# A two-layer transformer step: splits moved from GpSimd to VectorE, norm scales moved into the choice of experts, and gathered expert rows put into one buffer pool with the streamed table

## The chip, the cores and the metric

The kernel runs on one core of one Trainium2 chip. The metric is the device time of one execution in microseconds. The engines are named as in the profile: PE (TensorE matmul), PEld (its weight load), DVE (VectorE), ACT (ScalarE), POOL (GpSimd), SP (SyncE, which issues most DMAs).

## The reference, cut to what matters

Two layers work on 256 latent rows and 256 context rows of width 1024. Layer 0 mixes by attention and retention, layer 1 by a delta rule. After each mixer comes a layer norm and then `peer`: a lookup of 16 experts out of 16384 for each row and each of 8 heads, and after it another layer norm. `peer` is where most of the time goes:

```python
def block(xb):                                    # 128 rows
    q = (xb @ w_q).reshape(128, 8, 2, 128)
    s1, s2 = q[:, :, 0] . k1, q[:, :, 1] . k2     # 128 keys each
    v1, i1 = top_k(s1, 16); v2, i2 = top_k(s2, 16)
    cand = v1[..., :, None] + v2[..., None, :]
    sc, j = top_k(cand, 16)
    e_idx = ...                                    # 16 experts of i1 * 128 + i2
    gate = softmax(sc)
    act = gelu(einsum('phkd,pd->phk', u_tab[e_idx], xb))
    return einsum('phk,phkd->pd', gate * act, v_tab[e_idx])

xl = layer_norm(ALPHA * xl + g1 * yl, ln1_g[l], ln1_b[l])
fl = peer(modulate(xl, sh2, sc2), ...)
xl = layer_norm(ALPHA * xl + g2 * fl, ln2_g[l], ln2_b[l])
```

All of it is float32. The kernel gets that precision from float32r matmuls by splitting each operand x into a high part h = round(x) and a low part l = x - h, and adding three products (hh, hl, lh).

## The kernel before, in words

**Splits.** `split` writes the high part on ACT (tile names end in h: `arwh`, `ush`, `vsh`, `gsh`) and the low part by a subtraction with two SBUF operands on DVE or POOL (`arwl`, `usl`, `vsl`, `gsl`).

**First mixer** (0 to 190 us). 16 weight tiles `arw` and 4 tiles `rvw` are loaded, split and multiplied with the modulated input. Their low parts are computed on POOL (`eng=nc.gpsimd`). Beside them DVE computes `ada_unit`: the modulation vectors, one dot product of a 128x1024 tile with the condition for each of two streams (`adaj`, 48 of them here). `weave` interleaves the generators; the last part, `ret_v`, runs by itself after them. `w_out` is split on DVE and POOL in turn, and the modulated inputs (`hp0l`) alternate between the two too.

**Choice of experts** (`route`, 377 to about 700 us in layer 0; 2160 to 2370 us in layer 1). The query weights `wq` and the first chunks of table u are split on POOL here. DVE does the top-16 searches. The result is a dense weight table `wd` that goes through memory, and for row block 3 of layer 0 a list of expert numbers.

**Dense part of layer 0** (`Dense.run`, 716 to 1708 us). The tables u and v are streamed as 128 chunks of 128 experts. In the program's order each chunk c has: the load `ur` (512 KB) and its split, the product `act` with the activations, a `gelu`, the multiplication with the weights `w4`, its split `gsl`; the load `vr` (512 KB), its split `vsl`, and the product `f`. The first 36 chunks had their `act` done during the choice, so from 716 to 885 us there is only f. These are three of the four row blocks.

**Row block 3 of layer 0** goes another way: `Rows.steps` takes the 128 chosen experts of every row one at a time. For each of 128 steps POOL issues an indirect DMA of 512 KB from u (`rowu`, one expert row for each of 128 rows), DVE makes its dot product with the activations (`rowu`, then a read of the accumulator, `rowa`); 8 steps later (LAG) POOL gathers the same expert's row of v (`rowv`) and DVE adds it with its weight to the sum (`rowy`). A step is: multiply rowu s, issue gather of rowu s+RING[0], issue gather of rowv s-LAG+RING[1], add rowv s-LAG. The u rows have a ring of 4 buffers and the v rows one of 3 (RING = 4, 3), each its own; the `vr` chunks have 2 of the same size.

**The order.** The dictionary `fill` says at which chunk a step of the rows, an ada unit of layer 1 or something else is put; `at(share)` turns a share of the cost of all chunks into a chunk number. The scheduler that builds the program sets each engine's order and gives buffers to tiles as they are released in that order. `affine`, put at share 0.4, multiplies and adds the scale and shift of the first norm to x on POOL (lines 425 and 426 of the kernel before); layer 1 has another one at chunk 2.

Of the kernel before, what the change touches and what calls it, by code (L numbers as in the profile page):

```python
# [10 lines left out]
F32 = mybir.dt.float32  # L11
# [4 lines left out]
AF = mybir.ActivationFunctionType  # L16
# [5 lines left out]
P = 128  # L22
D = 1024
KD = D // P
# [22 lines left out]
AHEAD = 1  # L47
RING = 4, 3
LAG = 8
# [193 lines left out]
class Model:  # L243
# [186 lines left out]
    def modulate(self, pool, ps, l, m, x, s, hs, i0, ln):  # L430
        nc = self.nc
        sl = slice(i0 * P, (i0 + 2) * P)
        g, b = (self.c["ln_c"][:, ln[0], ln[1] - 1, z, :] for z in range(2))
        sc = pool.tile([P, KD], F32, tag="msc", name=f"msc{l}{m}{s}", bufs=2)
        sh = pool.tile([P, KD], F32, tag="msh", name=f"msh{l}{m}{s}", bufs=2)
        nc.vector.tensor_mul(sc, self.mod[l, m + 1][:, :, s], g)
        nc.vector.tensor_mul(sh, self.mod[l, m + 1][:, :, s], b)
        nc.vector.tensor_add(sh, sh, self.mod[l, m][:, :, s])
        for k in range(KD):
            self.n += 1  # L440
            o = ps.tile([P, 512], F32, tag="ps", name=f"xt{self.n}")
            for i in range(2):
                nc.tensor.transpose(o[:, i * P:(i + 1) * P], x[2 * s + i][:, k * P:(k + 1) * P], self.c["ident"])
            t = pool.tile([P, T], F32, tag="hf", name=f"hf{self.n}", bufs=3)
            nc.vector.tensor_scalar(t, o[:, :T], sc[:, k:k + 1], sh[:, k:k + 1], ALU.mult, ALU.add)
            nc.scalar.copy(hs[0][:, k, sl], t)
            (nc.gpsimd if k % 2 else nc.vector).tensor_sub(hs[1][:, k, sl], t, hs[0][:, k, sl].bitcast(F32))

# [19 lines left out]
    def mixer0(self, open_x, open_h):  # L468
# [25 lines left out]
        def weights(src, shape, nm):  # L494
            w = pw.tile(shape, F32, tag="w", name=nm, bufs=2)
            nc.sync.dma_start(w, src)
            return self.split(pw, w, shape, "arw", eng=nc.gpsimd)

# [120 lines left out]
        with ExitStack() as e2:  # L619
            pa = self.pool(e2, "m0ada2", 1, side="right")  # L620
            self.silu_rows(pa)

            def units():
                for m in (2, 3, 4):
                    for k in range(KD):
                        self.ada_unit(pa, 0, m, k, (0, 1))
                        yield

            weave(low(), pipe([key()] + [ret_proj(j) for j in range(4, 16)], 2), units())
            weave(ret_v())  # L630
        ep.close()
# [142 lines left out]
        with ExitStack() as e2:  # L774
            p = self.pool(e2, "m0o", 1, side="right")
            w = []
            for k in range(KD):
                r = p.tile([P, D], F32, tag="woutr", name=f"woutr{k}", bufs=3)
                nc.sync.dma_start(r, a["ar_out"][:, k, :])
                w.append(self.split(p, r, [P, D], f"wout{k}", eng=nc.gpsimd if k % 3 == 2 else nc.vector))  # L780
                next(rest, None)
# [30 lines left out]

    def route(self, l, hs, parts, ps, first, dense, e2, rows=None):
        nc, a, c = self.nc, self.a, self.c
# [15 lines left out]
        kT = p.tile([P, 16, P], F32, tag="A", name=f"kT{l}")  # L830
        nc.sync.dma_start(kT, a["p_k"][l])

        def top16(pool, vals, v, i, n, nm):
# [11 lines left out]
        def step(n):  # L845
            for _ in range(n):
                next(beside, None)
# [41 lines left out]
        def choose(part):  # L889
            n = 0  # L890
            pr = pipe([project(part, j) for j in range(16)], 2)
            for _ in range(2 * AHEAD):
                next(pr)
                yield
            tp = chain.from_iterable(top(part, j) for j in range(16))
            while True:
                ends = [next(g, pr) is pr for g in (pr, tp)]
                if all(ends):
                    return
                if ends[0]:  # L900
                    n += 1
                    step(1 + n % 2)
                yield

# [109 lines left out]
        for part in range(len(parts)):  # L1014
            weave(choose(part))
        eq_.close()
        dense.by = None
# [15 lines left out]
    class Rows:  # L1033
# [22 lines left out]

        def steps(self, pool):
            m, nc = self.m, self.m.nc
# [3 lines left out]
            def gather(z, s):  # L1062
                if 0 <= s < P:
                    t = rows[z, s] = pool.tile([P, D], F32, tag="row" + "uv"[z], name=f"row{'uv'[z]}{s}", bufs=RING[z])
                    nc.gpsimd.indirect_dma_start(t, None, tabs[z], bass.IndirectOffsetOnAxis(ap=self.e[:, s:s + 1], axis=0))  # L1065
# [20 lines left out]
    class Dense:  # L1086
# [61 lines left out]
        def run(self, wd, pool, psa, psv, fill, sums=None, ready=None):  # L1148
# [6 lines left out]
            def fetch(c):  # L1155
                late = c >= NE - 2
                vr = (self.p if late else pool).tile([P, D], F32, tag="ur" if late else "vr", name=f"vr{l}{c}", bufs=2)
                nc.sync.dma_start(vr, m.a["p_v"][l, c])
                if KEEP <= c < done:
                    self.gelu(c, None)  # L1160
                return vr
# [502 lines left out]
def build(nc, tc, a, out, dbg=None, upto="all"):  # L1664
    es = ExitStack()
    with es:
# [38 lines left out]
        dense = m.Dense(m, 0, h, 3, *pools0, EARLY[0])  # L1705
        wd = m.route(0, h, ((0, 1, 2, 3),), ps, first, dense, e2, rows)
        ep.close()
        psa = m.pool(e2, "psa0", 2, PSUM)
        psm = Tags(psa, ps=(psa, "act", 2))
        pools = (m.pool(e2, "densew0", 1), psa, m.pool(e2, "psv0", 1, PSUM))  # L1710
        steps = rows.steps(m.pool(ed, "rowring", 1, side="right"))
        ea = ExitStack()
# [3 lines left out]
        fill = {}  # L1716
        cost = np.cumsum([18 if c < EARLY[0] else 36 for c in range(NE - 6)])

# [6 lines left out]
        for i, u in enumerate(units):  # L1725
            n = 3 * KD
            share = ahead_share * (0.1 + 0.9 * i / n) if i < n else ahead_share + (0.97 - ahead_share) * (i - n) / (len(units) - n)
            fill.setdefault(at(share), []).append(lambda u=u: m.ada_unit(pa, *u))
        kept = {}

        def affine():
            rows = m.norm_rows(pa, 0, 1, "adat")
            for t in x[:4]:
                m.affine(nc.gpsimd, t, rows)

# [3 lines left out]

        fill.setdefault(at(0.4), []).append(affine)  # L1740
        fill[0] = [lambda: m.silu_rows(pa)]
        fill[124] = [prepare]
        for i in range(P + LAG):
# [5 lines left out]

        pm = Tags(m.pool(ed, "mod1", 1, side="right"), lnz=(pools[0], "w4", 2), hf=(pools[0], "vr", 2))  # L1750
        m.norm_modulate(pm, psm, (0, 2), (1, 0), x, (0, 1), ys, kept, h)
# [13 lines left out]
        with ed:  # L1765
            ep, ps = phase("r1ps")
            dense = m.Dense(m, 1, h, 2, *pools1, EARLY[1])
            wd = m.route(1, h, ((0, 1),), ps, first, dense, e2)
            ep.close()
# [6 lines left out]

            def affine():
                rows = m.norm_rows(pn, 1, 1)
                for t in x[2:4]:
                    m.affine(nc.gpsimd, t, rows)  # L1780

            last = dense.run(wd, *pools, {2: [affine]})
            for tb in range(2):
# [20 lines left out]
```

## Time and profile before

| | us |
|---|---|
| median of 3 runs | 3058.61 (3046.81 to 3059.09) |
| profiled execution, its own time | 3056.68 |
| its span, first to last instruction | 3054.9 |
| PE busy | 2773.7 (91%) |
| DVE busy | 2249.5 (74%) |
| ACT busy | 1291.4 (42%) |
| POOL busy | 643.4 (21%) |

The span is taken from the profile of one execution, whose own time is 1.8 us longer. PE's 91% is an average: the stages have different limits. A chunk of the dense part is about 8 to 9 us, and 128 of them make a third of the span.

### The profile page before, as it was taken

How to read it: one execution, taken by the hardware profiler on the slowest of the kernel's cores; microseconds unless marked ns; L12 is line 12 of the kernel's file. 1: busy time of each engine (PE TensorE's matmuls, PEld its weight loads, DVE VectorE, ACT ScalarE, POOL GpSimd, SP SyncE). 2: the span in 40 equal slices, each digit the busy share in tenths (PEclk: the TensorE clock that was granted, in tenths of full speed). 3: DMA queues.
4: the chain of work that ended last, by engine and by line, in shares of the span. 5: the costliest groups of instructions: out<-in, count | busy, mean ns of one | idle time of the engine just before them, and what ended most of it. 6: DMA issues, size and time to landing. Idle time of an engine off the chain costs nothing.

```text
span 3054.9 us, 44722 instructions
## 1 busy us (share of the span) xinstructions
PE 2773.7 (91%) x16867; PEld 2412.5 (79%) x16867; DVE 2249.5 (74%) x4414; ACT 1291.4 (42%) x2176; POOL 643.4 (21%) x413
## 2 busy tenths in 40 slices
PE   7988898987999789999999899678878899999997
PEld 4766788986788688888899677667877689999996
DVE  2976599796999898999744578876898655555555
ACT  3335333674333233333333356333457454444443
POOL 2410134001036765666100000122400100000000
PEclk9999899998999999999999899788999999999999
DMA  6531223668999799999744123313348866666763
GB/s 231 186 121 45 95 89 109 232 236 318 325 360 390 284 400 374 394 397 395 250 153 135 57 73 94 91 56 119 117 152 296 262 221 207 215 213 207 214 206 110
DMA packets 272168, 643.85 MB, mean 211 GB/s; under 512 B 36464, under 2 KB 138992, under 8 KB 267472
## 3 DMA queue, kind: packets, MB, share of 16 engines
q1 hardware_dynamic: 225120, 487.50, 47.7%
q0 software_dynamic: 38768, 142.49, 12.0%
q10 hardware_dynamic: 8064, 11.01, 1.0%
q8 instruction: 132, 2.16, 0.3%
q14 instruction: 84, 0.69, 0.1%
HBM read 583.77 MB, written 57.15 MB: 210 GB/s over the span
## 4 chain that ended last, share of the span: by engine, by line
PE 35%; DVE 13%; issue 9%; DMA 8%; POOL 5%; ACT 3%; POOLq 0%; DVEq 0%; ACTq 0%; SPq 0%
PE f L254 14%; PE act L254 13%; DMA rowv<-p_v,rowe 3%; PE dz L254 3%; DMA vr<-p_v 2%; POOL rowv L1065 2%; POOL rowu L1065 2%; DMA ur<-p_u 1%; DVE usl L271 1%; DVE vsl L271 1%; DVE cv L1332 1%; DVE rowu L1072 1%; PE qb L254 1%; DVE adaj L341 1%; DVE rowy L1082 1%
## 5 line engine op out<-in xcount | busy, mean ns | idle before, releaser
L254 PE MATMUL f<-vsl,gsh 128*128 128x512 f32 x1260 | 498.2, 397 | 29.2 <-DVE vsl L271 29.1
L254 PE MATMUL f<-vsh,gsh 128*128 128x512 f32 x1260 | 488.8, 397 | 23.7 <-ACT vsh L268 11.9
L254 PE MATMUL f<-vsh,gsl 128*128 128x512 f32 x1260 | 494.2, 394 | 7.0 <-DVE gsl L271 7.0
L271 DVE TENSOR_TENSOR vsl<-vr,vsh 128x1024 fp32r<-128x1024 f32 x252 | 304.2, 1239 | 193.9 <-ACT vsh L268 193.4
L271 DVE TENSOR_TENSOR usl<-ur,ush 128x1024 fp32r<-128x1024 f32 x240 | 293.8, 1225 | 182.4 <-ACT ush L268 180.8
L268 ACT ACTIVATE ush<-ur 128x1024 fp32r<-128x1024 f32 x256 | 270.3, 1056 | 268.5 <-PE act L254 165.9
L254 PE MATMUL act<-hp0h,usl 128*128 128x384 f32 x1024 | 348.1, 340 | 19.2 <-DVE usl L271 12.4
L254 PE MATMUL act<-hp0h,ush 128*128 128x384 f32 x1024 | 349.1, 341 | 3.6 <-ACT ush L268 3.3
L254 PE MATMUL act<-hp0l,ush 128*128 128x384 f32 x1024 | 346.7, 339 | 0.0
L268 ACT ACTIVATE vsh<-vr 128x1024 fp32r<-128x1024 f32 x252 | 257.6, 1053 | 207.9 <-PE f L254 141.1
L268 ACT ACTIVATE gsh<-gelu 128x384 fp32r<-128x384 f32 (+1 forms) x256 | 120.4, 471 | 490.7 <-DVE gelu L1172 380.7
L254 PEld LDWEIGHTS f<-vsl,gsh 128*128 128x128 f32 x1260 | 240.1, 191 | 85.9 <-DVE vsl L271 39.5
L254 PEld LDWEIGHTS f<-vsh,gsh 128*128 128x128 f32 x1260 | 238.6, 191 | 81.7 <-ACT vsh L268 22.8
L254 PE MATMUL act<-hp1h,usl 128*128 128x256 f32 x1024 | 292.6, 286 | 8.3 <-DVE usl L271 8.3
L254 PE MATMUL act<-hp1h,ush 128*128 128x256 f32 x1024 | 293.2, 286 | 1.3 <-ACT ush L268 1.2
L254 PE MATMUL act<-hp1l,ush 128*128 128x256 f32 x1024 | 292.3, 285 | 0.0
L254 PEld LDWEIGHTS f<-vsh,gsl 128*128 128x128 f32 x1260 | 240.0, 190 | 58.1 <-DVE gsl L271 8.4
L1065 POOL DMA_INDIRECT rowu<-p_ur,rowe x128 | 173.9, 1358 | 272.6 <-DVE rowa L1072 180.1
L254 PEld LDWEIGHTS act<-hp0h,usl 128*128 128x128 f32 x1024 | 195.0, 190 | 21.5 <-DVE usl L271 13.7
L1065 POOL DMA_INDIRECT rowv<-p_v,rowe x128 | 190.8, 1490 | 100.0 <-DVE rowy L1082 77.3
L254 PEld LDWEIGHTS act<-hp1h,usl 128*128 128x128 f32 x1024 | 198.4, 194 | 9.4 <-DVE usl L271 9.2
L254 PEld LDWEIGHTS act<-hp1h,ush 128*128 128x128 f32 x1024 | 198.7, 194 | 3.8 <-ACT ush L268 1.7
(777 smaller groups left out, 5810.8 us busy)
## 6 DMA issues: line engine op xcount, KB each, us to landing
ur<-p_u SPq DMA_DIRECT2D x256, 512.0 KB
vr<-p_v SPq DMA_DIRECT2D x256, 512.0 KB
adat<-ada_t SPq DMA_DIRECT2D x80, 512.0 KB
W<-wst SPq DMA_DIRECT2D x20, 2048.0 KB
w<-W SPq DMA_DIRECT2D x32, 768.0 KB
wq<-p_wq SPq DMA_DIRECT2D x32, 512.0 KB
dw<-dn_in SPq DMA_DIRECT2D x32, 512.0 KB
w<-W SPq DMA_DIRECT2D x32, 512.0 KB
```

Source lines behind the costliest of these rows:

```text
L254: self.nc.tensor.matmul(out, l, r, start=start, stop=stop)
L268: nc.scalar.activation(hi, x, AF.Copy)
L271: (eng or nc.vector).tensor_sub(lo, x, hi.bitcast(F32))
L341: nc.vector.tensor_tensor_reduce(j, w, self.crow[:, s, :], op0=ALU.mult, op1=ALU.add, scale=1.0, scalar=self.c["ada_c"][:, l, m, k:k + 1], ...
L1065: nc.gpsimd.indirect_dma_start(t, None, tabs[z], bass.IndirectOffsetOnAxis(ap=self.e[:, s:s + 1], axis=0))
L1072: nc.vector.tensor_tensor_reduce(u, u, self.h, op0=ALU.mult, op1=ALU.add, scale=1.0, scalar=0.0, accum_out=self.act[:, s:s + 1])
L1082: nc.vector.scalar_tensor_tensor(self.y, rows.pop((1, v)), self.g[:, v:v + 1], self.y, ALU.mult, ALU.add)
L1332: (nc.gpsimd if CONV[j] == "p" else nc.vector).scalar_tensor_tensor(co, xp[:, :ns, q:q + T], cw[:, j, q:q + 1], co, ALU.mult, ALU.add)
```

## The change

Seven edits, in the order of the program:

1. `weights` and `w_out` are split on DVE alone. The 24 ada units of the first mixer are no longer all run beside the projections: 16 are, and the other 8 beside `ret_v`.
2. In the modulate after a mixer, ACT computes the high part from PSUM itself, and all `hp` low parts go to DVE.
3. The scale and shift of the first norm (`affine`, both layers) moves into the choice of experts as `scaled`, one POOL operation at a time between the splits of `wq`.
4. RING goes from 4, 3 to 3, 2: gathers are issued one step later.
5. `rowu` and `rowv` no longer have rings of their own. They and the `vr` chunks of layer 0 share one tag, "vr", with 9 buffers (VRING; as many as the 4 + 3 + 2 before). The rows' steps are built with `pools[0]`.
6. The rows' steps and the ada units get other chunks: steps are spread over 126 chunks, not 122; the ada units end at 0.87 of the cost, not 0.97.
7. The `hf` tiles of the next modulate use the same 9 buffers.

```diff
-RING = 4, 3
+RING = 3, 2
+VRING = 9, 2
...
-            nc.scalar.copy(hs[0][:, k, sl], t)
-            (nc.gpsimd if k % 2 else nc.vector).tensor_sub(hs[1][:, k, sl], t, hs[0][:, k, sl].bitcast(F32))
+            nc.scalar.activation(hs[0][:, k, sl], o[:, :T], AF.Identity, bias=sh[:, k:k + 1], scale=sc[:, k:k + 1])
+            nc.vector.tensor_sub(hs[1][:, k, sl], t, hs[0][:, k, sl].bitcast(F32))
...
-            return self.split(pw, w, shape, "arw", eng=nc.gpsimd)
+            return self.split(pw, w, shape, "arw")
...
-            weave(low(), pipe([key()] + [ret_proj(j) for j in range(4, 16)], 2), units())
-            weave(ret_v())
+            sums = units()
+            weave(low(), pipe([key()] + [ret_proj(j) for j in range(4, 16)], 2), islice(sums, 2 * KD))
+            weave(ret_v(), until=sums, steps=3)
...
-                w.append(self.split(p, r, [P, D], f"wout{k}", eng=nc.gpsimd if k % 3 == 2 else nc.vector))
+                w.append(self.split(p, r, [P, D], f"wout{k}"))
...
+        def scaled():
+            gb = p.tile([P, 2, D], F32, tag="A", name=f"lgb{l}")
+            for i, z in enumerate("gb"):
+                nc.gpsimd.dma_start(gb[:, i, :], a[f"ln1_{z}"][l])
+            for t in x:
+                nc.gpsimd.tensor_mul(t, t, gb[:, 0, :])
+                yield
+                nc.gpsimd.tensor_add(t, t, gb[:, 1, :])
+                yield
...
+                if n % 4 == 0:
+                    next(scale, None)
...
-                    t = rows[z, s] = pool.tile([P, D], F32, tag="row" + "uv"[z], name=f"row{'uv'[z]}{s}", bufs=RING[z])
+                    t = rows[z, s] = pool.tile([P, D], F32, tag=tag, name=f"row{'uv'[z]}{s}", bufs=VRING[0])
...
-                vr = (self.p if late else pool).tile([P, D], F32, tag="ur" if late else "vr", name=f"vr{l}{c}", bufs=2)
+                vr = (self.p if late else pool).tile([P, D], F32, tag="ur" if late else "vr", name=f"vr{l}{c}", bufs=2 if late else VRING[l])
...
-        steps = rows.steps(m.pool(ed, "rowring", 1, side="right"))
+        steps = rows.steps(pools[0], tag="vr")
...
-        cost = np.cumsum([18 if c < EARLY[0] else 36 for c in range(NE - 6)])
+        cost = np.cumsum([18 if c < EARLY[0] else 36 for c in range(NE - 2)])
...
-            share = ahead_share * (0.1 + 0.9 * i / n) if i < n else ahead_share + (0.97 - ahead_share) * (i - n) / (len(units) - n)
+            share = ahead_share * (0.1 + 0.9 * i / n) if i < n else ahead_share + (0.87 - ahead_share) * (i - n) / (len(units) - n)
...
-        fill.setdefault(at(0.4), []).append(affine)
```

**The dense part of layer 0, DVE, chunks 92 and 93.** In the rows below the number behind a name is the tile's (gelu092 is chunk 92 of layer 0, rowu115 the gather of step 115). Before, DVE stood so:

```order
L1072 ISA rowu115_13020,rowa_2659<-rowu115_13020,rowh_2655 128x1024
L1072 ISA rowa_2659 128x1
L1172 TENSOR_TENSOR gelu092_12071<-gelu092_12071,w4092_12134 128x384
L271 TENSOR_TENSOR usl433_12193<-ur094_12190,ush433_12192 128x1024
L271 TENSOR_TENSOR gsl429_12138<-gelu092_12071,gsh429_12137 128x384
L1082 SCALAR_TENSOR_TENSOR rowy_2658<-rowv107_13121,rowg_2657,rowy_2658 128x1024
L1072 ISA rowu116_13119,rowa_2659<-rowu116_13119,rowh_2655 128x1024
L1072 ISA rowa_2659 128x1
L1172 TENSOR_TENSOR gelu093_12122<-gelu093_12122,w4092_12134 128x384
L271 TENSOR_TENSOR usl434_12239<-ur095_12236,ush434_12238 128x1024
L271 TENSOR_TENSOR gsl431_12147<-gelu093_12122,gsh431_12146 128x384
L1082 SCALAR_TENSOR_TENSOR rowy_2658<-rowv108_13160,rowg_2657,rowy_2658 128x1024
```

And now:

```order
L1101 SCALAR_TENSOR_TENSOR rowy_2658<-rowv91_12544,rowg_2657,rowy_2658 128x1024
L1091 ISA rowu100_12542,rowa_2659<-rowu100_12542,rowh_2655 128x1024
L1091 ISA rowa_2659 128x1
L272 TENSOR_TENSOR usl435_12168<-ur094_12165,ush435_12167 128x1024
L1191 TENSOR_TENSOR gelu092_12047<-gelu092_12047,w4092_12109 128x384
L272 TENSOR_TENSOR gsl431_12113<-gelu092_12047,gsh431_12112 128x384
L1091 ISA rowu101_12644,rowa_2659<-rowu101_12644,rowh_2655 128x1024
L1091 ISA rowa_2659 128x1
L1101 SCALAR_TENSOR_TENSOR rowy_2658<-rowv92_12646,rowg_2657,rowy_2658 128x1024
L1191 TENSOR_TENSOR gelu093_12097<-gelu093_12097,w4092_12109 128x384
L272 TENSOR_TENSOR usl436_12214<-ur095_12211,ush436_12213 128x1024
L272 TENSOR_TENSOR gsl433_12122<-gelu093_12097,gsh433_12121 128x384
```

The rows stand some 15 steps earlier in their list at the same chunk, and the two or four rows per pair of chunks lie among the same other work. What the order doesn't print is which buffer a gather takes. In the program as built before, rowu115 lies in the buffer that rowu111 left and rowv107 in that of rowv104. In the program as built now, rowu101 lies in the buffer that rowv91 leaves (the first row), rowv92 in that of rowu100, rowu102 in that of rowu101, rowv93 in that of rowv92, rowu103 in that of rowu102, rowv94 in that of rowv93, and the loads vr098 and vr099, issued on SP meanwhile, in those of vr091 and vr092.

**The first mixer, DVE.** `rq` and `rt` are the rotation of the queries. Before:

```order
L602 TENSOR_TENSOR rt6_661<-zr6_659,rsin_339 128x256
L603 TENSOR_TENSOR rq_96<-rq_96,rcos_338 128x256
L604 TENSOR_TENSOR rq_96<-rq_96,rt6_661 128x256
L341 ISA adaj0330_755,mod03_71<-adat033_753,c_row_351,small_58 128x1024
L341 ISA mod03_71 128x1
L341 ISA adaj0331_757,mod03_71<-adat033_753,c_row_351,small_58 128x1024
```

And now:

```order
L272 TENSOR_TENSOR arwl24_724<-arw9_721,arwh24_723 128x1024
L342 ISA adaj0301_669,mod03_71<-adat030_665,c_row_351,small_58 128x1024
L342 ISA mod03_71 128x1
L603 TENSOR_TENSOR rt6_661<-zr6_659,rsin_339 128x256
L604 TENSOR_TENSOR rq_96<-rq_96,rcos_338 128x256
L342 ISA adaj0310_705,mod03_71<-adat031_703,c_row_351,small_58 128x1024
```

The weight's split stands among the ada units, which are three units later than they were.

## Rows read from the trace of the kernel before

**Rows 1.** Window: length; PE, PEld, DVE, ACT, POOL busy us; PEclk; DMA share; GB/s.

```profile
885.00:1477.80 592.80, 552.57 (x2724) 495.96 (x2723) 542.40 (x722) 194.05 (x291) 366.12 (x250) 0.97 0.99 376
```

**Rows 2.** Windows, the splits vsl alone on DVE (one a chunk): count in brackets.

```profile
700.00:885.00 185.00, 43.53 (x36) 0.96 0.95 327
885.00:1477.80 592.80, 79.69 (x64) 0.97 0.99 376
1090.00:1477.80 387.80, 50.52 (x43) 0.98 1.02 388
1477.80:1569.20 91.40, 13.14 (x12) 1.00 0.57 182
```

**Rows 3.** Chain, tail of the dense part: start us, us, what.

```profile
1494.44 8.20 PE f L254 x36
1502.64 8.34 PE act L254 x48
```

**Rows 4.** Lines of DVE by form, 1100 to 1460 us.

```profile
L1082 DVE SCALAR_TENSOR_TENSOR rowy<-rowv,rowg,rowy 128x1024 f32<-128x1024 f32 x77 | 98.9, 1285 | 9.5 <-DMA rowv<-p_v,rowe 9.0 <-DVE rowg L1079 0.5
L1072 DVE CUSTOM_DVE_ANT_0 rowu<-rowu,rowh 128x1024 f32<-128x1024 f32 x77 | 94.0, 1221 | 0.0
L271 DVE TENSOR_TENSOR vsl<-vr,vsh 128x1024 fp32r<-128x1024 f32 x42 | 49.5, 1221 | 0.0
L341 DVE CUSTOM_DVE_ANT_0 adaj<-adat,c_row,small 128x1024 f16<-128x1024 f32 x19 | 24.3, 1279 | 0.0
L1172 DVE TENSOR_TENSOR gelu<-gelu,w 128x384 f32<-128x384 f32 x40 | 22.2, 555 | 7.0 <-ACT gelu L1137 7.0
```

**Rows 5.** Chain, pieces that end with a gather's landing.

```profile
958.50 12.51 DMA rowv<-p_v,rowe
...
1025.90 5.24 DMA rowv<-p_v,rowe
...
1451.44 7.66 DMA rowv<-p_v,rowe
...
1469.41 6.15 DMA rowv<-p_v,rowe
```

**Rows 6.** Timeline of DVE and of POOL near 1470 us: start, us, idle before.

```profile
1467.86 1.28 DVE L1082 SCALAR_TENSOR_TENSOR rowy<-rowv,rowg,rowy 128x1024 f32<-128x1024 f32 x1
...
1475.59 1.28 DVE L1082 SCALAR_TENSOR_TENSOR rowy<-rowv,rowg,rowy 128x1024 f32<-128x1024 f32 x1 [2.98 <-DMA rowv<-p_v,rowe]
...
1469.41 1.01 POOL L1065 DMA_INDIRECT rowv<-p_v,rowe  x1 [5.49 <-DVE rowy L1082]
```

**Rows 7.** Timeline of POOL and DVE at the norm's scales of layer 0.

```profile
1049.86 13.13 POOL L426 TENSOR_TENSOR x<-x,lb 128x1024 f32<-128x1024 f32 x4 [5.12 <-DMA lb<-ln_b]
...
1070.68 1.28 DVE L1082 SCALAR_TENSOR_TENSOR rowy<-rowv,rowg,rowy 128x1024 f32<-128x1024 f32 x1 [9.90 <-DMA rowv<-p_v,rowe]
```

**Rows 8.** Windows of first mixer, choice of layer 0, dense part of layer 1.

```profile
110.00:130.00 20.00, 19.77 (x87) 16.04 (x87) 19.54 (x28) 4.61 (x6) 7.56 (x3) 1.00 0.48 162
400.00:480.00 80.00, 79.46 (x410) 68.45 (x409) 79.41 (x550) 24.45 (x36) 28.80 (x12) 1.00 0.26 84
2370.00:2470.00 100.00, 84.76 (x377) 66.28 (x376) 63.26 (x87) 43.00 (x63) 9.82 (x4) 0.95 0.76 241
```

**Rows 9.** Lines by form: first mixer, DVE (70 to 190 us) and POOL (20 to 200 us).

```profile
L341 DVE CUSTOM_DVE_ANT_0 adaj<-adat,c_row,small 128x1024 f16<-128x1024 f32 x48 | 79.1, 1648 | 13.5 <-ACT c_row L330 12.3 <-DMA adat<-ada_t 0.6
L603 DVE TENSOR_TENSOR rq<-rq,rcos 128x256 f32<-128x256 f32 x4 | 5.4, 1348 | 0.0
L603 DVE TENSOR_TENSOR rk<-rk,rcos 128x256 f32<-128x256 f32 x4 | 5.4, 1346 | 0.0
...
L604 DVE TENSOR_TENSOR rk<-rk,rt 128x256 f32<-128x256 f32 x4 | 1.7, 414 | 0.0
...
L271 POOL TENSOR_TENSOR arwl<-arw,arwh 128x1024 fp32r<-128x1024 f32 x16 | 43.2, 2699 | 92.9 <-ACT arwh L268 85.6 <-PE z L254 7.3
L271 POOL TENSOR_TENSOR arwl<-rvw,arwh 128x1024 fp32r<-128x1024 f32 x4 | 10.8, 2711 | 15.3 <-ACT arwh L268 15.3
```

## What the change will do to the time

> **What bounds the kernel now.** I read the stages from the windows first, then the chain of waits in the stage where most of the edits land, then the lines and the timeline for durations.
>
> The stage is the dense part of layer 0 from chunk 36 on, where every chunk has both its products. In the 592.8 us of that window PE is busy 552.57 and DVE 542.40, POOL issues gathers, and the DMA share is 0.99 at 376 GB/s [rows 1]. The splits vsl, one to a chunk in the program's order, say how far the chunks are: 36 of them before 885 us, 64 from there to 1477.8, 12 more to 1569.2 [rows 2]. So chunks 36 to 111 take 1569.2 - 885 = 684 us.
>
> Two paces lie in it. When the gathered rows are done, the chain is PE alone: 8.20 + 8.34 = 16.54 us for two chunks, 8.27 a chunk [rows 3]. Before that, while DVE handles the rows, 43 splits take 387.8 us, 9.0 a chunk, with some edge; I take 8.9 [rows 2]. The reader is to see there that DVE is nearly full: beside a chunk's own splits (vsl 1.22 us, its twin usl the same, gelu 0.56, its twin gsl the same) it has a rowu of 1.22 and a rowy of 1.29 for each step and an ada unit of 1.28 [rows 4]. Yet the chain also goes through gathers: pieces of 5.24 to 12.51 us that end when a gather has landed [rows 5].
>
> **The change, part by part.**
>
> *The shared buffers (edits 4 and 5)* decide. In the program as built, I followed for each gather which buffer it takes and whose release that buffer waits for. The loads vr are issued by SP as soon as a buffer comes free, and they have no work between, so they come to hold more and more of the nine buffers: two at chunks 36 to 40, four at 44 to 52, six at 56 to 80, seven from 84 to 108. The rows are left with seven, five, three and then two, one for u and one for v. Before, they had four and three throughout. With two, a gather cannot be issued until DVE has consumed the step before. The order of DVE at chunks 92 and 93 shows it: rowu101 waits for the rowy of rowv91, rowv92 for rowu100, rowu102 for rowu101, rowv93 for rowv92, and between the release and the use there stand only a usl, a gelu and a gsl, 2.3 us, or nothing. DVE executes in order, so behind the waiting rowu stand the splits usl and vsl of the next chunks, and PE waits for those.
>
> What one such serial gather costs: the row op that uses it, 1.3 us [rows 4]; from its end to the issue of the next gather on POOL about 0.3 us (the rowy that starts at 1467.86 runs 1.28; POOL issues at 1469.41) [rows 6]; and from issue to use D. D is in the trace only where DVE waited: 5.24 us at the least, 6.15 at 1469 us, 7.66, and 12.51 where most transfers run [rows 5]. The rowy at 1475.59 waits 2.98 us for a gather issued at 1469.41, with a lead like those that the change has everywhere [rows 6]. I take D = 6.0: a little below the one at 1469 us, since the stage will move fewer bytes a microsecond than the 376 GB/s of now [rows 1] if it gets longer. A serial gather is then 6.0 + 0.3 + 1.3 = 7.6 us.
>
> Counting the longest chain of such gathers in each stretch of the built program (each use followed back to the release that its gather waits for): chunks 36 to 44 have 5, 44 to 56 have 9, 56 to 72 have 18, 72 to 84 have 16, 84 to 112 have 42 (1.5 a chunk; before it was 0.5 all along). The longer of the chain and of the other bounds counts:
> - 36 to 44: DVE 8 x 8.9 = 71 (gathers 38).
> - 44 to 56: DVE 107 (gathers 68), and 5 for leads that fall short here and there: 112.
> - 56 to 72: DVE 142, gathers 137. So near each other they add; I take 152.
> - 72 to 84: gathers 16 x 7.6 = 122 (PE 12 x 8.27 = 99).
> - 84 to 112: gathers 42 x 7.6 = 319 (PE 28 x 8.27 = 232).
>
> Sum 776, against 684: **+92**. With D = 5.24 a gather is 6.84 and the sum 71 + 107 + 142 + 109 + 287 = 716, +32; with 7.66 it is 9.26 and 71 + 112 + 167 + 148 + 389 = 887, +203.
>
> The Trainium skill ("DMA: Bandwidth & Descriptors", section "Anatomy of one DMA — SWDGE (gpsimd) path") speaks for a shorter gather: it gives about 2.0 us plus the bytes over 436 GB/s for one DMA, an estimate of 3.2 us for 512 KB. By it a serial gather would be 3.2 + 0.3 + 1.3 = 4.8 us, 42 of them 202 us, below PE's 232, and nothing would stall; that is the first rival below. The trace does not agree: no gather that DVE waited for took under 5.24 us [rows 5].
>
> *The scales of the norm out of the dense part (edit 3).* In layer 0, POOL's four additions block the gathers behind them for 13.13 us, and a rowy then waits 9.90 us [rows 7]. That stall goes, and is in the 684 but not in the 776. In the choice, eight such operations run beside a DVE that is busy 79.41 of 80 us with PE at 79.46 [rows 8]; most of DVE's work there has one input and does not slow, and a few two-input operations wait for one POOL operation each: +3, bounds 0 to 10. In layer 1, POOL's 9.82 us leave a window where PE is busy 84.76 of 100 [rows 8]; four DVE operations no longer wait 1 to 2 us each behind them: -3, bounds -6 to 0.
>
> *Rows and units at other chunks (edit 6).* Three rowu and one ada unit fewer stand before chunk 36, where DVE is the bound: 3 x 1.22 + 1.28 = 4.9 [rows 4], -5. The rest is in the sums above.
>
> *The first mixer (edit 1).* DVE is its bound: 19.54 of 20 us [rows 8]. It takes over 20 splits, 20 x 1.22 = 24.4 us (by vsl's row) [rows 4]. What it gets back is the slowing beside POOL's 54 us [rows 9]: the 48 ada operations have a mean of 1.648 us where the same form takes 1.279 in the dense part, 17.7 us; eight multiplications with rcos take 1.35 us where the one with rt takes 0.41, 7.5 us [rows 4, 9]. That is 25 against 24, about even. Eight of 24 units, 16 x 1.28 = 20.5 us, move from where DVE is the bound to beside ret_v. That has only four weight tiles [rows 9], so I count a third as covered: -6, bounds -12 and, if nothing is covered and the first weights come late, +2.
>
> *The rest* (w_out, edit 2, edit 7): two subtractions more on DVE for each pair of tiles, ACT no longer behind DVE. +-1, taken as 0.
>
> Sum: 92 + 3 - 3 - 5 - 6 = +81. The profiled execution took 3056.7 us, its span 3054.9, and it is 2 us below the median of 3058.6. 3056.7 + 81 = 3138, which I round to **3138 us**.
>
> **The rivals.**
> - *Faster: no gather stalls.* If loads and gathers land early enough that two buffers are enough, chunks 36 to 72 take 36 x 8.9 = 320 and 72 to 112 take 40 x 8.27 = 331, as DVE then has less than PE in every chunk (fewer rows a chunk, no ada). 651 against 684 is -33, with the other terms -44: 3013 us. For it speaks that most gathers of before land without anyone waiting: 9.0 us of idle time before 77 rowy [rows 4]. Against it: they have three or four buffers, and by the order and these durations 12 to 17 us of DVE work between release and use, while those of the changed program have 2 to 4 us. The same mechanism decides between the signs: with the other terms at -11, the stage must not lose more than 11, so 58 gathers may take 376 us, 6.5 each, D = 4.9. That is under every wait in the rows.
> - *About even.* D is 4.6 to 5.2 in a stage that is less loaded: 695 us or so for the stage, 3045 to 3070.
> - *Much slower.* The gathers stay as slow as where they are slowest among the chain's later ones, 7.66 us or more, since each of them still shares the DMA engines with loads that run far ahead: +203 - 11, 3249 us.
> - *The buffers' edit does not matter, the mixers' do.* Then the stage keeps 684 and the rest gives -11: 3046. It would need the rows to keep the buffers that they had, which the built program excludes.
>
> **How the numbers follow.** A measurement of this kernel can tell about 0.5%, 15 us, from no change. The forecast (D from 5.2 to 7.4, 3075 to 3225) has 0.75, much slower 0.10, about even 0.08, faster 0.07. The range of 8 in 10 runs from 3062, into the even case, to 3225, below the slowest. Slower by over 0.5% means above 3074: 0.85; within 0.5%: 0.08; faster: 0.07.
>
> **What would show it.** In the changed profile: waits of rowu and rowy on their gathers of some 100 to 250 us in sum, most of them after chunk 72, where 77 rowy of before waited 9.5 us [rows 4]; the splits vsl 11 to 12 us apart from chunk 84 to 112 and 8.9 before chunk 56; PE idle there for DVE's usl and vsl, and its granted clock lower in that stretch; the ada operations of the first mixer at 1.28 us and its end some 6 us earlier; no POOL stall near chunk 50. Wrong would be: splits 8.3 us apart to the end (faster), or a gap between gather and use of under 4.9 us as a rule.

## The result and the profile after

The changed kernel takes 3197.22 us, the median of 4 runs (3192.75 to 3203.09), against 3058.85 us before in runs beside it: a ratio of 1.046 (1.0434 to 1.0487). It is slower by 138 us, of which 81 were forecast. The profiled execution took 3192.75 us, 136 above that of before.

The page's busy times before and now (engine, us, share of the span, instructions) say first that nobody has more work:

```profile
PE 2773.7 (91%) x16867; PEld 2412.5 (79%) x16867; DVE 2249.5 (74%) x4414; ACT 1291.4 (42%) x2176; POOL 643.4 (21%) x413
...
PE 2826.9 (89%) x16867; PEld 2446.1 (77%) x16867; DVE 2242.7 (70%) x4456; ACT 1286.6 (40%) x2176; POOL 534.8 (17%) x371
```

DVE has as much as before, POOL 109 us less. PE is busy 53 us longer with the same 16867 matmuls. So the time went into waits, or into a slower PE. The splits vsl of the changed kernel, by stretch (window, length, busy us with the count, PEclk, DMA share, GB/s), show where. A window's edge counts a split on either side, so the counts run one or two over:

```profile
713.70:869.90 156.20, 43.63 (x36) 0.99 0.96 335
869.90:947.00 77.10, 9.76 (x9) 1.00 0.98 358
947.00:1066.80 119.80, 13.87 (x12) 0.96 0.97 359
1066.80:1244.50 177.70, 18.91 (x18) 0.89 0.88 312
1244.50:1381.80 137.30, 14.15 (x14) 0.90 0.78 262
1381.80:1720.70 338.90, 32.96 (x30) 0.89 0.69 229
```

These are chunks 0 to 35, 36 to 43, 44 to 55, 56 to 71, 72 to 83 and 84 to 111. From chunk 36 to 111 it is 850.8 us, where it was 685.4; the pace goes from 9.6 us a chunk to 12.1, and it does so stretch by stretch, as the loads vr come to hold more buffers. Chunks 0 to 35 on the other hand went from 168.8 us to 156.2. The same view of the kernel before, chunks 0 to 35 and 36 to 111:

```profile
716.20:885.00 168.80, 43.52 (x36) 0.96 0.95 327
885.00:1570.40 685.40, 93.94 (x76) 0.98 0.93 350
```

The column PEclk is the granted clock, 1.00 for 2.4 GHz. It was 0.98 in this stage and is 0.89 from chunk 56 on, so part of the time there is at 1.2 GHz. PE's 53 us fit that; no step of the chain of waits that is followed below runs through PE, and the clock is back at 0.99 in the first run below, with the waits gone. What the clock adds by itself was not measured.

What DVE waits for in chunks 36 to 111 of the changed kernel is in the idle time behind the bar (lines of DVE by form, 870 to 1720 us; the last row is that of the kernel before, 885 to 1570 us):

```profile
L1101 DVE SCALAR_TENSOR_TENSOR rowy<-rowv,rowg,rowy 128x1024 f32<-128x1024 f32 x122 | 156.6, 1284 | 190.7 <-DMA rowv<-p_v,rowe 190.6
L1091 DVE CUSTOM_DVE_ANT_0 rowu<-rowu,rowh 128x1024 f32<-128x1024 f32 x122 | 148.9, 1221 | 59.5 <-DMA rowu<-p_ur,rowe 59.5
...
L1082 DVE SCALAR_TENSOR_TENSOR rowy<-rowv,rowg,rowy 128x1024 f32<-128x1024 f32 x128 | 166.7, 1302 | 34.2 <-DMA rowv<-p_v,rowe 33.5 <-DVE rowg L1079 0.5
```

250 us of waits for gathers, where rowy had 33.5 before and rowu none.

Of the 136 us, +165 are in chunks 36 to 111 (forecast +92), -13 in chunks 0 to 35 (-5), -12 up to the choice of experts and +10 in it (-6 and +3), and about -14 behind (-3).

### The profile page after: what moved, and what is told of

Its sections match the earlier page's. It is cut to its first block, busy times and chain, and to the rows that moved or that the text cites. A ratio compares the mean times of both kernels' runs of the same rounds, so it can differ in the third digit from the quotient of the medians.

```text
span 3191.0 us, 44640 instructions
## 1 busy us (share of the span) xinstructions
PE 2826.9 (89%) x16867; PEld 2446.1 (77%) x16867; DVE 2242.7 (70%) x4456; ACT 1286.6 (40%) x2176; POOL 534.8 (17%) x371
## 5 line engine op out<-in xcount | busy, mean ns | idle before, releaser
L255 PE MATMUL f<-vsl,gsh 128*128 128x512 f32 x1260 | 510.6, 407 | 80.7 <-DVE vsl L272 80.4
L255 PE MATMUL f<-vsh,gsh 128*128 128x512 f32 x1260 | 498.8, 404 | 11.3 <-ACT vsh L269 6.8
L255 PE MATMUL f<-vsh,gsl 128*128 128x512 f32 x1260 | 503.0, 401 | 0.0
L255 PE MATMUL act<-hp0h,usl 128*128 128x384 f32 x1024 | 360.5, 352 | 71.7 <-DVE usl L272 65.2
L255 PE MATMUL act<-hp0h,ush 128*128 128x384 f32 x1024 | 358.0, 350 | 4.9 <-ACT ush L269 4.9
L255 PE MATMUL act<-hp0l,ush 128*128 128x384 f32 x1024 | 355.4, 347 | 0.0
L1101 DVE SCALAR_TENSOR_TENSOR rowy<-rowv,rowg,rowy 128x1024 f32<-128x1024 f32 x128 | 164.3, 1284 | 202.4 <-DMA rowv<-p_v,rowe 202.2
L1084 POOL DMA_INDIRECT rowu<-p_ur,rowe x128 | 165.4, 1292 | 523.1 <-DVE rowy L1101 182.4
L255 PEld LDWEIGHTS act<-hp0h,ush 128*128 128x128 f32 x1024 | 202.5, 198 | 7.3 <-ACT ush L269 5.5
L255 PEld LDWEIGHTS act<-hp0l,ush 128*128 128x128 f32 x1024 | 201.6, 197 | 1.8
```

Source lines behind the costliest of these rows:

```text
L255: self.nc.tensor.matmul(out, l, r, start=start, stop=stop)
L1101: nc.vector.scalar_tensor_tensor(self.y, rows.pop((1, v)), self.g[:, v:v + 1], self.y, ALU.mult, ALU.add)
```

## The experiments

Each time is compared with runs of the kernel before on the same chip (3054 to 3063 us in the median). The three runs given without a ratio were timed twice only; what they are to tell apart is far larger.

**Own rings again.** The changed kernel with the buffers as before:

```diff
-RING = 3, 2
-VRING = 9, 2
+RING = 4, 3
+VRING = 2, 2
...
-                    t = rows[z, s] = pool.tile([P, D], F32, tag=tag, name=f"row{'uv'[z]}{s}", bufs=VRING[0])
+                    t = rows[z, s] = pool.tile([P, D], F32, tag="row" + "uv"[z], name=f"row{'uv'[z]}{s}", bufs=RING[z])
```

> The changed kernel with the buffers as before: rowu in a ring of 4, rowv in one of 3, vr in 2; all other edits stay. Theory A (the loads vr come to hold the shared buffers, so that a gather waits for the row before it): the stage of chunks 36 to 111 falls from 851 us to 685 or less (the stall of the norm's scales, some 20 us, is gone too), the whole to 3005 to 3035 us, waits of rowu and rowy on gathers from 262 us to under 60. Rival B (the new chunks of the rows and units, or DVE's new work, made it slower): still above 3130 us. Rival C (gathers only take longer beside deep loads of vr): also near 3020, told apart by the third run.

Measured: 3023.86 us, ratio 0.9869 (0.984 to 0.9898). Chunks 36 to 111 of this run (the same columns as above), and its waits there:

```profile
878.60:1544.60 666.00, 89.76 (x77) 0.99 0.95 358
```

```profile
L1101 DVE SCALAR_TENSOR_TENSOR rowy<-rowv,rowg,rowy 128x1024 f32<-128x1024 f32 x128 | 163.7, 1279 | 24.0 <-DMA rowv<-p_v,rowe 24.0
L1091 DVE CUSTOM_DVE_ANT_0 rowu<-rowu,rowh 128x1024 f32<-128x1024 f32 x119 | 144.7, 1216 | 0.0
```

666 us and 24 us of waits: the whole loss goes, the granted clock is 0.99, and what is left is a kernel 39 us faster than before. Rival B (the new chunks, or DVE's new work) falls.

**Sharing alone.** The kernel before with edits 4, 5 and 7:

```diff
-RING = 4, 3
+RING = 3, 2
+VRING = 9, 2
...
-        steps = rows.steps(m.pool(ed, "rowring", 1, side="right"))
+        steps = rows.steps(pools[0], tag="vr")
```

> The kernel before with the shared pool of 9 and RING 3, 2 alone (edits 4, 5, 7). Theory A: about as much slower as the changed kernel's dense part, +150 to +190 us, 3200 to 3250. Rival B: within 15 us of before.

Measured: 3198.59 us, ratio 1.0453 (1.0409 to 1.0496): +135, a little under the range given. Chunks 36 to 111 take 841 us. The shared pool by itself makes the change's loss. With the other edits in place it costs more, 173 us, from the 3023.86 of the run above to 3197.22.

**The rows share among themselves.** The changed kernel with one ring of 7 for rowu and rowv and 2 buffers for vr:

```diff
-VRING = 9, 2
+VRING = 2, 2
+ROWS = 7
...
+                    t = rows[z, s] = pool.tile([P, D], F32, tag=tag, name=f"row{'uv'[z]}{s}", bufs=ROWS)
...
+        steps = rows.steps(pools[0], tag="row")
```

> The changed kernel, but rowu and rowv share 7 buffers among themselves and vr has 2 of its own. Theory A: sharing among the rows costs nothing, since nobody else can take their buffers: 3000 to 3035 us, as the run with own rings. Rival D (it is the taking in turn of u and v that serialises the gathers, not the loads of vr): above 3120 us.

Measured: 3020.96 us, ratio 0.9871 (0.9834 to 0.9908). Chunks 36 to 111 take 659 us. Taking buffers in turn is no harm as long as only the gathers take them. Rival D falls.

**Sharing with the gathers one step earlier.** The changed kernel with one line of its own:

```diff
-RING = 3, 2
+RING = 4, 3
```

> The changed kernel with RING 4, 3 in place of 3, 2, buffers shared as in the change: gathers are asked for one step earlier in program order. Theory A: the buffer's release decides, not the place in the order: 3170 to 3205 us. Rival E (a gather issued one step later is what lacks): under 3100 us.

Measured: 3194.52 us, ratio 1.0428 (1.0392 to 1.0465). The place of a gather in the program is worth nothing when it waits for a buffer. Rival E falls.

**Two buffers for the rows from the start, with vr in seven, and in two.** Both are the changed kernel with the tag "row" as above; the first:

```diff
-VRING = 9, 2
+VRING = 7, 2
+ROWS = 2
```

and the second:

```diff
-VRING = 9, 2
+VRING = 2, 2
+ROWS = 2
```

> The changed kernel with fixed shares: rowu and rowv have two buffers from the start, vr seven, which is what the shared pool ends in. Theory A: the slow pace of the changed kernel's chunks 84 to 112 (12.1 us a chunk) holds from chunk 36 to the end; by the built program 112 serial gathers at about 8.1 us up to chunk 112, so about 900 us there against 666 with own rings, and 50 more behind it: 3290 to 3370 us. Rival B (something else in the late part is slow): near 3200.

> As the run with two buffers for the rows, but vr has two, not seven. Theory A: few buffers for the rows are the whole cost, deep loads of vr neither help nor hurt: within 25 us of that run. Rival C (loads running far ahead slow the gathers' transfers): clearly faster than that run, by 60 us or more.

Measured: 3304.84 and 3304.81 us. Chunks 0 to 35 and 36 to 111 with vr in seven:

```profile
714.60:871.80 157.20, 43.71 (x36) 0.96 0.95 330
871.80:1793.90 922.10, 89.70 (x78) 0.90 0.73 250
```

and with vr in two:

```profile
712.80:882.30 169.50, 43.43 (x36) 0.97 0.93 317
882.30:1803.60 921.30, 89.61 (x77) 0.88 0.72 246
```

922 and 921 us: it is the two buffers of the rows that cost, and loads that run far ahead do not slow the gathers beside them. Rival C falls. The first lines tell the other side: with seven buffers for vr, chunks 0 to 35 take 157.2 us, with two 169.5. There the loads do gain. 922 us for 76 chunks are 12.1 us each, the pace of the changed kernel from chunk 84 on; for the 112 serial gathers of that program they are 8.2 us each.

**Half rows.** Every gather brings 256 KB, and half of block 3's sum is left out:

```diff
-            tabs = m.a["p_ur"], m.a["p_v"][0].rearrange("n p d -> (n p) d")
+            tabs = m.a["p_ur"].rearrange("n (h d) -> (n h) d", h=2), m.a["p_v"][0].rearrange("n p (h d) -> (n p h) d", h=2)
...
+                    t = rows[z, s] = t[:, :D // 2]
```

> The changed kernel, but every gather brings half a row (512 of 1024 columns, from the first half of the table) and the row operations on DVE work on 512 columns, so half of block 3's sum is left out and the rest is of other rows; this measures what a gather's time is made of. Theory A with a gather of 5.7 us, of which about 1.9 are bytes: a serial gather falls by 0.9 + 0.6 us to 6.5, the stage to about 740 us, the whole to 3060 to 3110 us. If the gather were nearly all bytes: below 3010. If none of it were bytes: 3150 to 3180.

Measured: 3179.76 us, outside the range given for the theory and at the value given for a gather in which bytes count nothing. But the run does not measure that as it was meant to. The build hands the buffers out in another way: in chunks 36 to 111 POOL waits 35 times, 219 us in sum, for the split of a vr load before it can issue a gather (the idle time on the first row below is one of them), where the changed kernel has 11 such waits of 19 us, and the stretches are slow from chunk 36 on (98.5 us for chunks 36 to 43, not 77.1). POOL's issues of two rowu of this run and their uses on DVE (start, us, idle before):

```profile
1488.55 1.68 POOL L1085 DMA_INDIRECT rowu<-p_ur,rowe  x1 [7.90 <-DVE vsl L272]
...
1493.71 1.69 POOL L1085 DMA_INDIRECT rowu<-p_ur,rowe  x1 [2.23 <-DVE rowa L1092]
```

```profile
1492.74 0.69 DVE L1092 CUSTOM_DVE_ANT_0 rowu<-rowu,rowh 128x512 f32<-128x512 f32 x1 [3.33 <-DMA rowu<-p_ur,rowe]
...
1498.60 0.69 DVE L1092 CUSTOM_DVE_ANT_0 rowu<-rowu,rowh 128x512 f32<-128x512 f32 x1 [2.40 <-DMA rowu<-p_ur,rowe]
```

From issue to use it is 4.19 and 4.89 us. The 39 rowu that DVE waited for between 1400 and 1700 us took 5.0 in the mean, and 13 whole rows in chunks 84 to 111 of the changed kernel 5.45; for rowv there is no gain (6.1 in the mean of 11, and 6.0 of 42). So half of the bytes are worth half a microsecond or nothing, and bytes are the smaller part of a gather; the theory's 1.9 us of bytes, 0.9 for the half, shows in no run. What the saving would be with the buffers handed out as in the change stays open.

**The first mixer alone.** The kernel before with edits 1 and 2 (two of their lines):

```diff
-            return self.split(pw, w, shape, "arw", eng=nc.gpsimd)
+            return self.split(pw, w, shape, "arw")
...
-            weave(ret_v())
+            weave(ret_v(), until=sums, steps=3)
```

> The kernel before with edits 1 and 2 alone (splits of the first mixer, of w_out and of the modulate on DVE, eight ada units beside ret_v). The prediction's step says -6 us (bounds -12 to +2), the changed kernel's own trace says -12 up to the choice: 3046 to 3058 us, the ada operations at 1.28 us. Rival (DVE is the bound there and its 24 us of new splits are paid): +10 to +20 us.

Measured: 3046.56 us, ratio 0.9961 (0.9945 to 0.9978), -12 us. The mixer's last product with a split weight, `rvp`, last starts at 174.2 us and not at 186.5, so all of it is won there. The ada operations of this run, 1.648 us in the mean before [rows 9]:

```profile
L341 DVE CUSTOM_DVE_ANT_0 adaj<-adat,c_row,small 128x1024 f16<-128x1024 f32 x48 | 61.4, 1278 | 4.5 <-ACT c_row L330 3.5 <-DMA adat<-ada_t 0.8
```

**The scales alone.** The kernel before with edit 3 (`scaled` in the choice, no `affine`):

> The kernel before with edit 3 alone (the first norm's scales in the choice). The prediction's steps: choice +3, layer 0's dense part some -20 (the POOL stall), layer 1's -3; the changed kernel's trace says +10, -20 and -12. So 3035 to 3048 us. Rival (the stall is only moved, since DVE and PE are full in the choice): within 8 us of before.

Measured: 3035.43 us, ratio 0.9929 (0.9904 to 0.9954), -23 us. In the choice it loses. POOL's timeline of this run (start, us), and PE's line of the query product that uses the split (350 to 420 us):

```profile
381.14 4.75 POOL L839 TENSOR_TENSOR x<-x,lgb 128x1024 f32<-128x1024 f32 x2 [4.25 <-DMA lgb<-ln_g]
385.85 4.64 POOL L841 TENSOR_TENSOR x<-x,lgb 128x1024 f32<-128x1024 f32 x2
390.46 2.33 POOL L839 TENSOR_TENSOR x<-x,lgb 128x1024 f32<-128x1024 f32 x1
392.76 2.33 POOL L271 TENSOR_TENSOR usl<-wq,ush 128x1024 fp32r<-128x1024 f32 x1
```

```profile
L254 PE MATMUL pq<-hp0h,usl 128*128 128x512 f32 x44 | 18.8, 426 | 9.9 <-POOL usl L271 9.9
```

The order of the built program lets the scales run ahead of the splits of wq on POOL. The first usl starts at 392.76 behind five scale operations in three rows, and PE, which needs it, waits 9.9 us. The split of chunk 0 starts at 727.9 us, where it was 716.2. In the dense part of layer 0 the stall [rows 7] is gone: chunks 36 to 111 take 661 us, where it was 685.

In the changed kernel the same scales cost in another way. There edit 2 has put the subtractions `hp0l` of the modulate on DVE, and the scales run beside them on POOL. DVE, POOL and then PE's lines from 350 to 420 us of the changed kernel:

```profile
355.99 6.41 DVE L448 TENSOR_TENSOR hp0l<-hf,hp0h 128x256 fp32r<-128x256 f32 x3
...
363.68 6.26 DVE L448 TENSOR_TENSOR hp0l<-hf,hp0h 128x256 fp32r<-128x256 f32 x3
```

```profile
354.81 4.83 POOL L841 TENSOR_TENSOR x<-x,lgb 128x1024 f32<-128x1024 f32 x2 [3.22 <-ACT x L422]
359.60 5.01 POOL L843 TENSOR_TENSOR x<-x,lgb 128x1024 f32<-128x1024 f32 x2
364.58 5.08 POOL L841 TENSOR_TENSOR x<-x,lgb 128x1024 f32<-128x1024 f32 x2
```

```profile
L255 PE MATMUL pq<-hp0h,ush 128*128 128x512 f32 x68 | 28.1, 414 | 7.7 <-ACT hp0h L447 7.7
...
L255 PE MATMUL pq<-hp0h,usl 128*128 128x512 f32 x68 | 27.0, 397 | 0.0
```

The same DVE rows in the run with the first mixer alone, which has edit 2 and not the scales:

```profile
358.58 1.15 DVE L447 TENSOR_TENSOR hp0l<-hf,hp0h 128x256 fp32r<-128x256 f32 x3
...
361.01 1.14 DVE L447 TENSOR_TENSOR hp0l<-hf,hp0h 128x256 fp32r<-128x256 f32 x3
```

Six subtractions take 12.7 us beside the scales and 2.3 without them. The next high parts come later by that, and PE waits 7.7 us for them, where it waits 2.2 in the run with the first mixer alone. For the split usl it does not wait at all.

**Early loads shared, later ones not.** From the two runs with two buffers follows a version that has both gains: the first 36 loads of vr take their buffers with the rows (7), those from chunk 36 on have 2 of their own.

```diff
-VRING = 9, 2
+VRING = 7, 2
...
-                vr = (self.p if late else pool).tile([P, D], F32, tag="ur" if late else "vr", name=f"vr{l}{c}", bufs=2 if late else VRING[l])
+                vr = (self.p if late else pool).tile([P, D], F32, tag="ur" if late else "vr" if c < done else "vw", name=f"vr{l}{c}", bufs=VRING[0] if not l and c < done else 2)
```

> The changed kernel, but only the first 36 loads of vr share with the rows (7 buffers in one tag); from chunk 36 on vr has a tag of 2 of its own, so that the rows keep all 7. Theory A: chunks 0 to 35 keep the 12 us that deep loads of vr gained there (157 against 169 us in the runs with two rows' buffers and vr 7 or 2), and chunks 36 to 111 keep the 666 us of own rings: 3005 to 3020 us, under the run with own rings (3024) by 5 to 15. Rival: the buffers that early loads take come free too late for the first rows, chunks 36 to 56 lose what the early ones gain: 3024 or more.

Measured: 3007.11 us, ratio 0.9828 (0.9802 to 0.9855), with both kernels beaten. Its chunks 0 to 35 and 36 to 111:

```profile
708.80:871.00 162.20, 43.71 (x36) 0.98 0.93 325
871.00:1531.70 660.70, 89.73 (x77) 0.99 0.96 364
```

162 and 661 us: of the 12 us of the early chunks about half are kept beside the gain of own rings (chunks 0 to 35 took 168 there).

**The scales later.** The same version, with the scales' table in memory that comes free after the last query product, so that POOL cannot run them ahead of wq:

```diff
-                if n % 4 == 0:
-                    next(scale, None)
...
-        weave(scale)
         eq_.close()
+        pgb = self.pool(es, "lgb", 1)
...
             decode(part)
+            weave(scale)
```

> The version with early loads shared (3007 us), with the norm's scales allowed only after the last query product, so that POOL runs them among its splits of the first chunks of u and not ahead of those of wq. Theory F (in the choice, PE waited 9.9 us for two splits of wq that stood behind the scales in POOL's queue): 8 to 12 us under that version, 2995 to 3000. Rival G (the scales cost the same wherever they stand, since DVE's two-input operations wait beside them): within 4 us of it.

> The version with early loads shared once more, on the same chip as the run beside it: 3004 to 3012 us by every theory.

Measured: 3025.63 us, ratio 0.9895 (0.9875 to 0.9915), against 3006.74 us, 0.9836 (0.9813 to 0.986), for the version without it. That is 19 us slower and neither theory's figure. POOL's timeline of the run with late scales (lines 841 and 843 are the scales), and PE's lines of the product that uses the split usl from 460 to 520 us, of it and of the version without:

```profile
503.66 5.23 POOL L843 TENSOR_TENSOR x<-x,lgb 128x1024 f32<-128x1024 f32 x2
508.84 5.14 POOL L841 TENSOR_TENSOR x<-x,lgb 128x1024 f32<-128x1024 f32 x2
513.95 2.78 POOL L272 TENSOR_TENSOR usl<-ur,ush 128x1024 fp32r<-128x1024 f32 x1
```

```profile
L255 PE MATMUL act<-hp0h,usl 128*128 128x384 f32 x52 | 19.9, 382 | 20.4 <-POOL usl L272 20.4
```

```profile
L255 PE MATMUL act<-hp0h,usl 128*128 128x384 f32 x63 | 22.7, 360 | 6.3 <-POOL usl L272 6.3
```

PE waits 20.4 us for POOL's splits there and not 6.3: the splits of u now stand behind the scales. Theory F started from a wait that the version without does not have: its PE, like that of the changed kernel above, waits 7.7 us for the high parts and 0.0 for the splits of wq. The late scales do bring the 7.7 down to 2.2, and lose more in their new place. At the split of chunk 0 the run is 9 us behind, at that of chunk 112 10 us; the rest comes in layer 1, whose scales stand later too, and is not taken apart.

## Why the prediction was right, point by point

*The mechanism* held in each part. The loads vr take the buffers from the rows, the rows end up with two, and each gather waits for the row before it: undone, the stage falls to 666 us; forced from the start, it takes 922; neither the deep loads, nor the place of the gathers, nor the taking in turn does it. The rivals "no gather stalls" and "the buffers' edit does not matter" are out by 180 and 150 us, "about even" (up to 3070) by 127, "much slower" (3249) by 50. Of the signs, the waits came (250 us, 183 of them from chunk 72 on), the splits 12.1 us apart from chunk 84 on, the lower clock and the ada operations at 1.28 us. The 8.9 us a chunk before chunk 56 did not: they are 9.6 and 10.0.

*Its size* was too small: +92 forecast, +165 measured. One reading was off by 1 us: the split of chunk 112, where the stretch ends, starts at 1570.4 and not at 1569.2. All five stretches are over their forecasts (us; DVE's busy time is that of the window, the waits are those of rowu and rowy for gathers):

| chunks | forecast | measured | DVE busy | waits for gathers |
|---|---|---|---|---|
| 36 to 43 | 71 | 77.1 | 65.4 | 2.8 |
| 44 to 55 | 112 | 119.8 | 99.6 | 20.2 |
| 56 to 71 | 152 | 177.7 | 133.7 | 43.8 |
| 72 to 83 | 122 | 137.3 | 90.0 | 47.0 |
| 84 to 111 | 319 | 338.9 | 194.3 | 136.4 |

Two steps of the sum were mis-sized. The first is "a serial gather is then 6.0 + 0.3 + 1.3 = 7.6 us", which lacks a term. The timeline of the changed kernel at chunks 92 and 93, DVE first (start, us, idle before with what ended it), then POOL:

```profile
1482.30 1.28 DVE L1101 SCALAR_TENSOR_TENSOR rowy<-rowv,rowg,rowy 128x1024 f32<-128x1024 f32 x1 [3.95 <-DMA rowv<-p_v,rowe]
1483.50 1.22 DVE L1091 CUSTOM_DVE_ANT_0 rowu<-rowu,rowh 128x1024 f32<-128x1024 f32 x1
...
1491.97 1.28 DVE L1101 SCALAR_TENSOR_TENSOR rowy<-rowv,rowg,rowy 128x1024 f32<-128x1024 f32 x1 [1.32 <-DMA rowv<-p_v,rowe]
...
1497.92 1.28 DVE L1101 SCALAR_TENSOR_TENSOR rowy<-rowv,rowg,rowy 128x1024 f32<-128x1024 f32 x1 [1.45 <-DMA rowv<-p_v,rowe]
...
1505.23 1.29 DVE L1101 SCALAR_TENSOR_TENSOR rowy<-rowv,rowg,rowy 128x1024 f32<-128x1024 f32 x1 [3.76 <-DMA rowv<-p_v,rowe]
```

```profile
1483.85 1.68 POOL L1084 DMA_INDIRECT rowu<-p_ur,rowe  x1 [5.83 <-DVE rowy L1101]
1485.83 1.31 POOL L1084 DMA_INDIRECT rowv<-p_v,rowe  x1 [0.30 <-issue]
...
1493.53 1.01 POOL L1084 DMA_INDIRECT rowv<-p_v,rowe  x1 [1.67 <-DVE rowy L1101]
...
1499.47 1.68 POOL L1084 DMA_INDIRECT rowv<-p_v,rowe  x1 [1.79 <-DVE rowy L1101]
```

From the rowy at 1482.30 to the one at 1505.23 two chunks pass in 22.93 us. The reader can follow the chain: the rowy ends and POOL issues a rowu at 1483.85; the rowv behind it in POOL's queue can only be issued at 1485.83, 1.98 us later (1.68 of the first issue and 0.30); that rowv is used at 1491.97 (6.14 after issue), the next is issued at 1493.53 and used at 1497.92 (4.39), the next issued at 1499.47 and used at 1505.23 (5.76). Three gathers of 5.4 in the mean, three times 1.55 from a use to the next issue, and once 1.98 us before the rowv: 16.29 + 4.66 + 1.98 = 22.93. The prediction had the first two terms and not the third. Its rowv takes the buffer of the rowu at 1483.50, which is free at 1484.72; so of the 1.98 us about 1.2 are that row operation, which stands on DVE behind the rowy, and 0.8 the queue of POOL behind the issue of the other gather.

This round is the shortest of the twelve from the rowy at 1407.26 to that at 1704.67, which take 24.78 us in the mean. With 4.66 and 1.98 taken off, a gather of the chain takes 6.05 us there: D was right. The twelve rounds take 297.4 us, where 36 gathers of 7.6 are 273.6, and the 23.8 between are twelve times the third term. The rounds differ by one gather. In every second one a table of weights for `gelu` (w, 768 KB) is loaded, and in all six of these the rowv issued just before it takes 6.81 to 7.50 us; in five of the other six it takes 4.33 to 4.80.

The second is "the longer of the chain and of the other bounds counts". In chunks 56 to 71 both are near each other; "I take 152", and 177.7 were measured. The table shows that DVE's work and its waits add up to the whole stretch there (133.7 + 43.8), and in the stretches on either side of it: a wait of one row is not filled by the work that stands behind it on the same engine. D was short there as well: the 21 gathers that DVE waited for in chunks 56 to 71 took 7.0 us in the mean, which makes the chain of 18 some 155 us by itself and leaves 23 for the adding. In chunks 36 to 43 DVE hardly waits for gathers, and what the 6 us over the forecast are is open.

The Trainium skill's rule for one DMA ("DMA: Bandwidth & Descriptors", section "Anatomy of one DMA — SWDGE (gpsimd) path", an estimate of 3.2 us for 512 KB) does not hold for these gathers: 4.39 to 6.14 us from the start of the issue to the use above, of which the issue itself is 1.0 to 1.7, and none that DVE waited for in chunks 36 to 111 took under 4.26.

*The other steps.* The first mixer was worth twice its term, -12 and not -6, the bound given; the ada operations came down to 1.278 us, as forecast. The scales in the choice cost 10 us and not 3, the upper bound, and at least in part by the way that the prediction named, two-input operations of DVE that wait beside POOL's: six subtractions lose 10.4 us, of which PE waits 5.5 more; where the rest of the 10 is lost is open. In the kernel before with the scales alone it was another way, PE's wait for a split. Layer 0's stall was rightly taken as gone. Chunks 0 to 35 gained 13 us and not 5: with vr in seven and in two they take 157.2 and 169.5 us, so the loads vr that run ahead there are worth 12 of the 13, and the forecast term, "three rowu and one ada unit fewer" (six rowu there now, nine before), about 1. The prediction saw these loads only as a cost. Behind chunk 111, -14 where -3 was forecast: a window of the changed kernel at the start of layer 1's dense part (us, then PE, PEld, DVE, ACT, POOL busy, PEclk, DMA) has PE busy 94.15 of 100, where the like one of before had 84.76 [rows 8], which is 9 us of it:

```profile
2505.00:2605.00 100.00, 94.15 (x470) 75.22 (x470) 60.96 (x90) 49.49 (x73) 0.00 (x0) 1.00 0.82 267
```

## What to carry to other kernels

Buffers in one pool go to whoever asks first. A stream of loads that has nothing to do but wait for a buffer takes most of them from a consumer whose next request depends on its own last result, and it gains nothing by that once its own bound lies elsewhere; share in the stretch where only the stream is active, and give the dependent requests their own ring where both run. When counting such a chain, count each engine's queue that a request passes through, the issuing engine's too, and every operation that stands ahead of a release, and add waits to the work of an in-order engine rather than taking the larger of the two. An operation moved to another engine is to be looked at with what runs beside it there in the same program: the scales cost one thing in the kernel before and another in the changed one.

## What had not been expected of the hardware

A gather of rowu took 5.0 us in the mean from issue to use with 256 KB and 5.45 with 512 KB, so most of it is not its bytes. A gather of 512 KB issued 0.2 us before a load of 768 KB took 6.8 to 7.5 us, in five of six rounds without that load 4.3 to 4.8. Seven buffers for the loads beside them or two made no difference to the gathers (922 and 921 us for the same chain). An issue of an indirect DMA holds POOL's queue for 0.94 to 1.7 us, and the next one starts 0.3 us later. Three subtractions of 128x256 with two inputs on DVE took 6.4 us beside POOL's multiplications of 128x1024, and 1.15 without them.
